# Moving operands read downward, x in tiles of 320 words, and one weight distance a pair, in a two-layer hybrid block on one core

## The chip, the cores and the metric

The kernel runs on one core of a Trainium2 chip. A core has five engines that run beside each other: TensorE (PE, matrix products; the load of a stationary operand is listed as PEld), VectorE (DVE), ScalarE (ACT), GpSimd (POOL) and SyncE (SP, which here only issues transfers). They work on SBUF, an on-chip memory of 128 partitions; PE writes its results to PSUM, which DVE and ACT read. Sixteen DMA engines move data between HBM and SBUF. The metric is the device time of one execution in microseconds (us), smaller being better; several executions are timed and the median is given.

## The reference

The reference is a small language-model block in float32: 256 tokens after 16 learned meta tokens, width 1024, two layers. Cut to what matters:

```python
for li in range(2):
    hn = rms_norm(h, norm_mix_g[li])
    proj = hn @ w_in[li]              # 1024 -> 13312, cut into 12 parts
    o = [retention(...), hgrn2(...), diff_attention(...)]       # each 1024 wide
    y = sum(sigmoid(gate[n]) * (o[n] @ w_branch[li][n]) for n in range(3))
    h = h + y @ w_out[li]
    hn = rms_norm(h, norm_ffn_g[li])
    u = hn @ w_ffn_in[li]                                       # 1024 -> 5632
    c = conv_b + sum(conv_w[j] * shifted(u, 2 - j) for j in range(3))
    gate, val = split(c, 2)
    h = h + (silu(gate) * val) @ w_ffn_out[li]                  # 2816 -> 1024
return rms_norm(h, norm_final_g)[:, meta tokens cut off]
```

Three sequence mixers work on parts of one wide projection; then come their output projections, and a gated feed-forward with a convolution over three tokens. Nearly all arithmetic is in the products with weights, 216 MB of them, each read once.

## The kernel before

**Layout.** Features lie on the 128 partitions and tokens along the free dimension, 272 of them (T). A weight tile is 128 x 128 and is the stationary operand of a product; activations are the moving operand, one column a token. In the second layer the pairs whose results only matter for the last 256 tokens (and two before them, for the convolution) work on 258 columns, from token 14 (T0); the pairs named in FULL keep 272.

**Three products a tile.** To keep float32 accuracy with the fast operand type float32r, each weight tile and each activation is split in two, a rounded part (hi) and the rest (lo). `products` (from line 845) issues for each weight tile three products into the same PSUM region: hi weights by hi activations (line 868), hi weights by lo activations (869) and lo weights by hi activations (870). The main products of all projections run through this function: the wide projection (names rq to m2, numbered in BASE), the branch outputs b0 to b2, wo, the feed-forward input fi (22 pairs j of two tiles) and output fo. The last layer's fo is different: there the weights are the moving operand, 512 columns at a time, and the activations (ghi, glo) the stationary one, so that tokens land on partitions (`final`, from line 1346; products in 1378 to 1380).

**Weights.** They come as a stream in the order of use, eight tiles (512 KB) a chunk. `_Weights.next` (class in line 558) issues the transfer of a chunk into wraw (three buffers), then one ACT instruction that writes whi and one DVE instruction that writes wlo (four buffers each). Where each tile begins in those buffers is worked out in `_places` (line 125): `wants` holds a byte offset, modulo LINE = 256 bytes, for every tile. It is the sum of APART (0, or 96 for pairs that work on 258 columns), 64 more for the branch, wo and fo tiles (BLOCK), and 64 times (k modulo 4), k being the number of the 128 features that are summed over. Gaps are left so that each tile begins there; `_runs` turns the result into strided access patterns. 

**Activations.** The normalised input x is held in six fixed tiles (`xs`, line 725): xh0, xh1, xh2 and xl0 to xl2, each with four k of 272 words. A tile k thus begins 1088 bytes after the one before, which is 64 modulo 256; the weight tiles' 64 bytes a k follow that. The other moving operands (b0hi, b0lo and the like in `split_blocks`, yhi and ylo, ghi and glo) lie in slots, buffers of 4 x 272 words of which there are 14 (SLOTS). Slots also hold q, k and v blocks of the mixers, scratch of the second mixer, and more. A slot tile is taken when it is first written and comes free after its last reader.

**Norms.** A norm's factor rstd is known only after all features are summed, so the first four pairs behind a norm use x without it and are multiplied by rstd afterwards (`evacuate`); for the fifth pair on, `Norm.next` writes x once more with rstd folded in: POOL writes y, ACT xh, DVE xl, for eight k. This happens four times.

**Order.** The program order is made when the kernel is built: every instruction is recorded with an estimated cost and a due time (`plan.key`), and `_Plan.order` picks instructions by readiness and due time, with the number of free buffers of each kind in view. Dependencies between instructions come from `_span`, which gives the range of words that an access pattern touches. The main products follow the fixed list ORDER; the small products of the mixers are woven in between.

Of the kernel before, what the change touches and what calls it, by code (L numbers as in the profile page):

```python
# [12 lines left out]
F32R = mybir.dt.float32r  # L13
# [6 lines left out]
P = 128  # L20
# [3 lines left out]
T = META + SEQ  # L24
D = 1024
KD = D // P
# [8 lines left out]
TAIL = T - 2 * P  # L35
BANK = 512
CHUNK_TILES = 8
SLOTS = 14
LEAD = 6.0
MARGIN = 12.0  # L40
EARLY = 12.0
# [6 lines left out]
BASE = {"rq": 0, "rk": 4, "rv": 8, "rg": 16, "hq": 24, "hf": 32, "hi": 40, "hg": 48,  # L48
        "dq": 56, "dk": 64, "dv": 72, "m0": 80, "m1": 88, "m2": 96}
# [67 lines left out]
LINE = 256  # L117
APART = (0, 96)
BLOCK = 64
ROOM = CHUNK_TILES * P + 2 * LINE // 4  # L120
T0 = META - 2
FULL = ("rk", "rv", "hf", "hi", "dk", "dv")


def _places(depth=DEPTH):

    wants = []
    for li in range(depth):  # L130
        for name, j, k, _ in sum(_turns(li), []):
            if name == "fo" and (li == DEPTH - 1 or j == 3):
                wants.append(None)
                continue
            short = li == DEPTH - 1 and name not in FULL
            wants.append(APART[short] + BLOCK * (name[0] == "b" or name in ("wo", "fo")) + 64 * (k % 4))
    out = []
    for c in range(0, len(wants), CHUNK_TILES):
        at, places = 0, []
        for want in wants[c : c + CHUNK_TILES]:  # L140
            if want is not None:
                at += (want // 4 - at) % (LINE // 4)
            places.append(at)
            at += P
        assert at <= ROOM
        out.append(places)
    return out


def _runs(places):  # L150


    runs = []
    for i, at in enumerate(places):
        if runs and at == runs[-1][1] + runs[-1][2] * P:
            runs[-1][2] += 1
        else:
            runs.append([i, at, 1])
    out = []
    for i, at, n in runs:  # L160
        if out and out[-1][4] == n and (out[-1][3] == 1 or at == out[-1][1] + out[-1][2] * out[-1][3]):
            if out[-1][3] == 1:
                out[-1][2] = at - out[-1][1]
            out[-1][3] += 1
        else:
            out.append([i, at, 0, 1, n])
    return out


def _rope_perm(d):  # L170
# [145 lines left out]
class _Plan:  # L316
# [25 lines left out]

    def _span(self, ap):
        step = ap.ap[0][0]
        lo = ap.offset % step
        hi = lo + 1 + sum((n - 1) * abs(s) for s, n in ap.ap[1:])
        if ap.tensor.name in self.psum:

            lo, hi = lo // BANK * BANK, -(-hi // BANK) * BANK
        return ap.tensor.name, lo, hi  # L350
# [261 lines left out]
def _trace(ctx, tc, plan, a, depth, probe):  # L612
# [9 lines left out]
    wp = ctx.enter_context(tc.tile_pool(name="wp", bufs=3))  # L622
    sp = ctx.enter_context(tc.tile_pool(name="sp", bufs=SLOTS))
    gp = ctx.enter_context(tc.tile_pool(name="gp", bufs=3))
# [11 lines left out]
    def fixed(shape, name, dt=F32):  # L636
        return new(cp, shape, dt, name, 1, name)

    def slot(name, dt=F32):
        return new(sp, [P, 4 * T], dt, "slot", SLOTS, name)  # L640

    def slot4(name, dt=F32):
        return slot(name, dt).rearrange("p (a t) -> p a t", a=4)
# [78 lines left out]
    fmap = fixed([P, DEPTH], "fmap")  # L722
    fixed([P, KD], "step")

    xs = [[fixed([P, KD // 2, T], f"x{n}{i}", F32R) for n in "hl"] for i in range(3)]

    def x_tile(k, folded):
        return tuple(t[:, k % 4, :] for t in xs[1 if k >= 4 else 2 if folded else 0])
    rstd = fixed([P, T], "rstd")


# [168 lines left out]
    def split(hi, lo, x):  # L900
        act.activation(hi, x, AF.Copy)
        tt(lo, x, hi.bitcast(F32), SUB)
# [30 lines left out]
    def split_blocks(name, blocks, t0):  # L933

        his, los = [], []
        for x in blocks:
            hi, lo = slot4(name + "hi", F32R), slot4(name + "lo", F32R)
            split(hi[:, :, t0:], lo[:, :, t0:], x[:, :, t0:])
            his.append(hi)
            los.append(lo)  # L940
        return lambda k: (his[k // 4][:, k % 4, :], los[k // 4][:, k % 4, :])

    for li in range(depth):
        last = li == depth - 1
# [15 lines left out]
        st = {}  # L960
# [441 lines left out]
        for name, j in ORDER:  # L1402
# [18 lines left out]
            elif name[0] == "*":  # L1421
                plan.key = clock[0] - MARGIN
                n = name[1:]
                if n == "b2":
                    blocks = [st["da0"], st["da1"]]
                else:
                    t = st["rg" if n == "b0" else "hg"]
# [6 lines left out]
            if name in BASE:  # L1434
                lo = 0 if name in FULL else t0
                ps = products(lambda k: x_tile(k, norm.folded), name, j, lo)
# [16 lines left out]
                elif name in ("dq", "dk"):  # L1453
                    t = block(f"{name}{j // 2}")
# [12 lines left out]
                elif name in ("hi", "dv"):  # L1467
                    n = name[0] + "v"
# [13 lines left out]
                else:  # L1482
                    t = block(f"{name}{j // 2}")
# [7 lines left out]
            elif name in ("b0", "b1", "b2"):  # L1491
                ps = products(st["x" + name], name, j, t0)
                g = st["m" + name[1]][:, both, t0:]
                yy = block(f"y{j // 2}")[:, two, t0:]
                if name == "b0":
                    tt(yy, ps, g, MUL)
                else:
                    tt(g, ps, g, MUL)
                    tt(yy, yy, g, ADD)
                    if name == "b2":  # L1500
                        if j == 0:
                            st["yhi"] = [slot4("yhi", F32R) for _ in range(2)]
                            st["ylo"] = [slot4("ylo", F32R) for _ in range(2)]
                        split(st["yhi"][j // 2][:, two, t0:], st["ylo"][j // 2][:, two, t0:], yy)
            elif name == "wo":
                hi, lo = st["yhi"], st["ylo"]
                ps = products(lambda k: (hi[k // 4][:, k % 4, :], lo[k // 4][:, k % 4, :]), name, j, t0)
                tt(h[:, both, t0:], h[:, both, t0:], ps, ADD)
                if j == 0:
                    norm = Norm(small[:, S_GF + li * KD : S_GF + (li + 1) * KD])  # L1510
                norm.take([2 * j, 2 * j + 1])
                norm.square([2 * j, 2 * j + 1])
                if j == 3:
                    norm.finish()
            elif name == "fi":
                ps = products(lambda k: x_tile(k, norm.folded), name, j, t0)
                if j % 4 == 0:
                    st.setdefault("ghi", []).append(slot4("ghi", F32R))
                    st.setdefault("glo", []).append(slot4("glo", F32R))
                u = ps  # L1520
                if not norm.folded:
                    u = temp2("two_a")[:, :, t0:]
                    evacuate(u, ps)
                first = META if last else 0
                c = temp2("two_b")
                for f in range(2):
                    ft = j + f * FK
                    w = lambda i: small[:, S_CW + (li * 3 + i) * 2 * FK + ft : S_CW + (li * 3 + i) * 2 * FK + ft + 1]
                    bias = small[:, S_CB + li * 2 * FK + ft : S_CB + li * 2 * FK + ft + 1]
                    act.activation(c[:, f, first:], u[:, f, first - t0 :], AF.Identity, bias=bias, scale=w(2))  # L1530
                    for back in (1, 2):
                        at = max(first, back)
                        stt(c[:, f, at:], u[:, f, at - back - t0 : T - back - t0], w(2 - back), c[:, f, at:], MUL, ADD)
                c = c[:, :, first:]
                act.activation(c[:, 0, :], c[:, 0, :], AF.Silu)
                tt(c[:, 0, :], c[:, 0, :], c[:, 1, :], MUL)
                split(st["ghi"][j // 4][:, j % 4, first:], st["glo"][j // 4][:, j % 4, first:], c[:, 0, :])
            elif last:
                if j == 0:
                    final()  # L1540
            else:
                hi, lo = st["ghi"], st["glo"]
                ps = products(lambda k: (hi[k // 4][:, k % 4, :], lo[k // 4][:, k % 4, :]), name, j)
                if j == 0:
                    norm = Norm(small[:, S_GM + (li + 1) * KD : S_GM + (li + 2) * KD])
                    le_set()
                for ks, x in ([([6], ps[0].unsqueeze(1)), ([7], ps[1].unsqueeze(1))] if j == 3 else [([2 * j, 2 * j + 1], ps)]):
                    if ks[0] == 6:
                        plan.key -= 22 * 0.35
                    if ks[0] == 7:  # L1550
                        norm.rest = True
                        norm.mean()
                        plan.key = clock[0] - 1.0
                    hk = h[:, ks[0] : ks[-1] + 1, :]
                    tt(hk, hk, x, ADD)
                    norm.square(ks)
                    norm.take(ks)
# [20 lines left out]
```

## Time and profile before

| | |
|---|---|
| median of 3 runs | 1329.39 us (1329.1 to 1330.91) |
| profiled execution, span from the first to the last instruction | 1327.6 us |
| PE busy | 1317.0 us, 99% |
| DVE busy | 962.7 us, 73% |
| ACT busy | 816.7 us, 62% |
| POOL busy | 83.6 us, 6% |
| HBM read | 216.16 MB, 164 GB/s over the span |

The profiled execution's own time is its span, and the median of the runs stands 1.8 us above it. A row of the view of groups reads: line, engine, operation, output <- inputs, partitions x elements, count | busy us in total, mean ns of one | idle time of that engine before them and what ended it. In a row of the view of windows stand the window, its length, and for each engine its busy time and in brackets how many instructions ran, then the granted PE clock, the busy share of the DMA engines and their GB/s. In the view of waits a row reads: who waited <- for whom: us in total, times, longest us. In the chain in order of time: start us, us, what. A row for one tile gives minimum, median and maximum duration in ns, then the first and the last start in us.

### The profile page before, as it was taken

What the parts mean: (1) busy time and instruction counts of PE and PEld (TensorE: products, weight loads), DVE (VectorE), ACT (ScalarE), POOL (GpSimd) and SP (SyncE); (2) the same over time, 40 slices, a digit from 0 to 9 for tenths busy, and PEclk for the clock granted to TensorE, in tenths of its full rate; (3) what the DMA queues carried; (4) which work ended last, traced back from release to release, by engine and by line L of the source; (5) the groups of instructions that cost most, each with busy time, mean ns of one, the idle gap of its engine ahead of it and who ended that gap; (6) DMA issues with size and microseconds to landing.
All of it is one profiled execution on the core that took longest, in us unless ns stands there. A gap on an engine that the chain in (4) does not pass through costs nothing.

```text
span 1327.6 us, 28926 instructions
## 1 busy us (share of the span) xinstructions
PE 1317.0 (99%) x11862; PEld 1288.8 (97%) x11862; DVE 962.7 (73%) x1630; ACT 816.7 (62%) x1374; POOL 83.6 (6%) x161
## 2 busy tenths in 40 slices
PE   9999999999999999999999999999999999999998
PEld 9999999999999999999999999999999999999986
DVE  7675777697586789886574757776985867898753
ACT  6747454756676567666456474557565775767643
POOL 5000000001010020000030000000011100200000
PEclk9999999999999999999999999999999999999999
DMA  7644543443534545555555445444445446465653
GB/s 272 195 146 155 170 150 128 143 143 129 188 131 158 177 157 176 187 168 186 175 175 181 155 159 161 160 140 143 143 149 175 142 162 199 135 208 189 201 182 109
DMA packets 60755, 219.07 MB, mean 165 GB/s; under 512 B 6864, under 2 KB 6992, under 8 KB 60624
## 3 DMA queue, kind: packets, MB, share of 16 engines
q1 hardware_dynamic: 60336, 216.71, 49.1%
q8 instruction: 93, 1.52, 0.5%
q10 hardware_dynamic: 288, 0.52, 0.1%
q14 instruction: 38, 0.31, 0.1%
HBM read 216.16 MB, written 1.05 MB: 164 GB/s over the span
## 4 chain that ended last, share of the span: by engine, by line
PE 95%; DVE 3%; issue 1%; DMA 0%; ACT 0%; SPq 0%; DVEq 0%
PE main L868 28%; PE main L870 27%; PE main L869 27%; PE fo L1380 2%; PE fo L1378 2%; PE fo L1379 2%; PE lev L1059 1%; DVE two_b L553 1%; PE ds L1243 1%; PE ms L553 1%; PE do L553 1%; DVE wlo L553 1%; PE ro L553 1%; PE ho L553 1%; PE vt L553 1%
## 5 line engine op out<-in xcount | busy, mean ns | idle before, releaser
L868 PE MATMUL main<-xh,whi 128*128 128x272 f32 (+1 forms) x2368 | 693.2, 293 | 0.2 <-ACT whi L553 0.2
L870 PE MATMUL main<-xh,wlo 128*128 128x272 f32 (+1 forms) x2368 | 680.5, 287 | 0.8 <-DVE wlo L553 0.7
L869 PE MATMUL main<-xl,whi 128*128 128x272 f32 (+1 forms) x2368 | 671.6, 284 | 1.6 <-DVE xl L553 1.5
L553 DVE TENSOR_TENSOR wlo<-wraw,whi 128x1024 fp32r<-128x1024 f32 (+1 forms) x408 | 497.1, 1223 | 200.9 <-ACT whi L553 199.8
L553 ACT ACTIVATE whi<-wraw 128x1024 fp32r<-128x1024 f32 (+1 forms) x408 | 426.6, 1048 | 229.5 <-PE main L869 162.2
L869 PEld LDWEIGHTS main<-xl,whi 128*128 128x128 f32 x2368 | 448.9, 190 | 2.5 <-DVE xl L553 2.1
L868 PEld LDWEIGHTS main<-xh,whi 128*128 128x128 f32 x2368 | 445.6, 188 | 2.5 <-issue 0.7
L870 PEld LDWEIGHTS main<-xh,wlo 128*128 128x128 f32 x2368 | 444.6, 188 | 2.2 <-DVE wlo L553 2.1
L553 DVE SCALAR_TENSOR_TENSOR two_b<-main,small,two_b 128x256 f32<-128x256 f32 (+2 forms) x144 | 65.3, 488 | 29.1 <-ACT two_b L553 27.4
L553 POOL TENSOR_TENSOR y<-h,rstd 128x272 f32<-128x272 f32 x32 | 34.6, 1114 | 316.7 <-ACT rstd L553 316.7
L553 ACT ACTIVATE two_b<-main,small 128x272 f32<-128x272 f32 (+1 forms) x72 | 37.3, 567 | 26.8 <-PE main L870 26.6
L870 PE MATMUL main<-ghi,wlo 128*128 128x272 f32 x176 | 51.0, 290 | 0.0
L868 PE MATMUL main<-ghi,whi 128*128 128x272 f32 x176 | 50.9, 289 | 0.0
L869 PE MATMUL main<-glo,whi 128*128 128x272 f32 x176 | 50.2, 285 | 0.0
L553 ACT ACTIVATE vsrc<-main 128x544 f32<-128x544 f32 x24 | 15.0, 626 | 39.4 <-PE main L870 39.2
L868 PE MATMUL main<-b0hi,whi 128*128 128x272 f32 (+1 forms) x128 | 38.1, 298 | 0.0
L868 PE MATMUL main<-b1hi,whi 128*128 128x272 f32 (+1 forms) x128 | 38.1, 298 | 0.0
L870 PE MATMUL main<-yhi,wlo 128*128 128x272 f32 (+1 forms) x128 | 36.7, 286 | 0.0
L870 PE MATMUL main<-b2hi,wlo 128*128 128x272 f32 (+1 forms) x128 | 36.6, 286 | 0.0
L870 PE MATMUL main<-b1hi,wlo 128*128 128x272 f32 (+1 forms) x128 | 36.6, 286 | 0.0
L870 PE MATMUL main<-b0hi,wlo 128*128 128x272 f32 (+1 forms) x128 | 36.6, 286 | 0.0
L868 PE MATMUL main<-yhi,whi 128*128 128x272 f32 (+1 forms) x128 | 36.5, 285 | 0.0
(244 smaller groups left out, 1936.4 us busy)
## 6 DMA issues: line engine op xcount, KB each, us to landing
wraw<-in_w SPq DMA_DIRECT2D x402, 512.0 KB, 3.4
h<-in_h SPq DMA_DIRECT2D x4, 272.0 KB, 5.2
dec<-in_dec SPq DMA_DIRECT2D x2, 544.0 KB, 5.4
wraw<-in_w SPq DMA_DIRECT2D x4, 256.0 KB, 4.6
const<-in_const SPq DMA_DIRECT2D x1, 937.0 KB, 6.1
gain<-in_gl SPq DMA_DIRECT2D x1, 512.0 KB, 6.1
out<-y ACTq DMA_DIRECT2D x2, 256.0 KB, 2.8
out<-y SPq DMA_DIRECT2D x2, 256.0 KB, 2.7
```

The source lines that it names most:

```text
L553: self.plan.add(self.name, lambda: f(*args, **kw), cost, outs, ins, args[2] if method == "activation" else None)
L868: nc.tensor.matmul(o, wh, hi, start=first, stop=False)
L869: nc.tensor.matmul(o, wh, lo, start=False, stop=False)
L870: nc.tensor.matmul(o, wl, hi, start=False, stop=last)
L1059: nc.tensor.matmul(o, keys, x, start=True, stop=True)
L1243: nc.tensor.matmul(ss[m][:, at : at + nk], q[half, hd, q0 : q0 + P], k[half, hd, :nk], start=True, stop=True)
L1378: nc.tensor.matmul(o, gh, wh, start=False, stop=False)
L1379: nc.tensor.matmul(o, gl, wh, start=False, stop=False)
L1380: nc.tensor.matmul(o, gh, wl, start=False, stop=end)
```

## The change

The x tiles get room for 320 words a k (WIDE), of which 272 are used, so that a k begins 1280 bytes after the one before, a multiple of 256. The weight tiles of the wide projection and of fi no longer step by 64 bytes a k; those of the wide projection begin at APART, and in fi each pair j has its own offset from a list (SPREAD): the multiples of 16 bytes up to 240, then six more from 8 on in steps of 40. The x tiles grow by 4608 bytes a partition; there is one slot of 4352 bytes less.

The new function `_down` makes an access pattern that goes through the last dimension from its end to its beginning. All moving operands of the main products are taken through it, where they are written (by ACT and DVE) and where they are read (by PE). The last token therefore lies at the lowest address, and PE reads from the highest address down. The stationary ghi and glo of the last stage stay as they were. `_span` is mended so that a negative step gives the right range.

```diff
-SLOTS = 14
+SLOTS = 13
...
+SPREAD = [16 * i for i in range(16)] + [8 + 40 * i for i in range(6)]
+WIDE = 320
...
+            if name in BASE or name == "fi":
+                wants.append((SPREAD[j] if name == "fi" else APART[short]) % LINE)
+                continue
             wants.append(APART[short] + BLOCK * (name[0] == "b" or name in ("wo", "fo")) + 64 * (k % 4))
...
+def _down(t):
+
+
+    step, n = t.ap[-1]
+    return bass.AP(t.tensor, t.offset + (n - 1) * step, [list(x) for x in t.ap[:-1]] + [[-step, n]])
...
-        lo = ap.offset % step
+        lo = ap.offset % step + sum((n - 1) * min(s, 0) for s, n in ap.ap[1:])
...
-    xs = [[fixed([P, KD // 2, T], f"x{n}{i}", F32R) for n in "hl"] for i in range(3)]
+    xs = [[fixed([P, KD // 2, WIDE], f"x{n}{i}", F32R)[:, :, :T] for n in "hl"] for i in range(3)]
 
     def x_tile(k, folded):
-        return tuple(t[:, k % 4, :] for t in xs[1 if k >= 4 else 2 if folded else 0])
+        return tuple(_down(t[:, k % 4, :]) for t in xs[1 if k >= 4 else 2 if folded else 0])
...
-            hi, lo = slot4(name + "hi", F32R), slot4(name + "lo", F32R)
+            hi, lo = (_down(slot4(name + n, F32R)) for n in ("hi", "lo"))
...
-                            st["yhi"] = [slot4("yhi", F32R) for _ in range(2)]
-                            st["ylo"] = [slot4("ylo", F32R) for _ in range(2)]
+                            st["yhi"] = [_down(slot4("yhi", F32R)) for _ in range(2)]
+                            st["ylo"] = [_down(slot4("ylo", F32R)) for _ in range(2)]
...
-                    st.setdefault("ghi", []).append(slot4("ghi", F32R))
-                    st.setdefault("glo", []).append(slot4("glo", F32R))
+                    for n in ("ghi", "glo"):
+                        t = slot4(n, F32R)
+                        st.setdefault(n, []).append(t if last else _down(t))
```

## The prediction

> **What bounds the kernel now.** I read the page first, its shares of busy time, the clock line and the shares of the chain that ended last:
>
> ```profile
> span 1327.6 us, 28926 instructions
> PE 1317.0 (99%) x11862; PEld 1288.8 (97%) x11862; DVE 962.7 (73%) x1630; ACT 816.7 (62%) x1374; POOL 83.6 (6%) x161
> PEclk9999999999999999999999999999999999999999
> PE 95%; DVE 3%; issue 1%; DMA 0%; ACT 0%; SPq 0%; DVEq 0%
> ```
>
> PE carries 95% of the chain, at full granted clock in all 40 slices. A busy PE may still wait inside, so the view of waits for PE alone comes next:
>
> ```profile
> PE main L869 <- DVE xl L553: 1.5, 1, 1.5
> PE warm L553 <- POOL ones_d L553: 1.0, 1, 1.0
> PE main L870 <- DVE wlo L553: 0.7, 3, 0.3
> PE lev L1059 <- issue: 0.5, 1, 0.5
> ```
>
> Nearly nothing: PE is the bound because it has work, and the time is the number of its products times the spacing of their starts. So I counted products. The view of groups with shapes kept apart, for line 869 (one of the three products of a weight tile; 868 and 870 have the same counts):
>
> ```profile
> L869 PE MATMUL main<-xl,whi 128*128 128x272 f32 x1536 | 437.3, 285 | 0.1
> L869 PE MATMUL main<-xl,whi 128*128 128x258 f32 x832 | 234.3, 282 | 1.5 <-DVE xl L553 1.5
> L869 PE MATMUL main<-glo,whi 128*128 128x272 f32 x176 | 50.2, 285 | 0.0
> L869 PE MATMUL main<-b0lo,whi 128*128 128x272 f32 x64 | 18.2, 285 | 0.0
> L869 PE MATMUL main<-b0lo,whi 128*128 128x258 f32 x64 | 18.0, 281 | 0.0
> ```
>
> b1, b2 and y have 64 of each shape as b0 has. So products of 272 columns: 3 x (1536 + 176 + 4 x 64) = 5904; of 258: 3 x (832 + 4 x 64) = 3264; together 9168. All of them get a moving operand that is read downward. One ns on each is 9.2 us, 0.69% of the time; 0.2%, about what a measurement of this kernel tells from no change, is 2.7 us or 0.29 ns a product.
>
> Their spacing is not their duration (285 ns; they overlap), but window length over count. Windows inside the stages that hold nothing else, first for line 869 alone (272 columns, then 258), then for the 512-column products of the last stage:
>
> ```profile
> 520.00:660.00 140.00, 106.24 (x375) 1.00 0.56 184
> 1165.00:1255.00 90.00, 70.64 (x251) 1.00 0.60 198
> 1260.00:1318.00 58.00, 57.79 (x251) 1.00 0.48 154
> ```
>
> 140/375/3 = 124.4 ns, 90/251/3 = 119.5 ns, 58/251 = 231 ns. What would they be if only columns counted? The fp32 products, which run as two passes each, tell. From the chain in order of time (four passes of 144 columns, two of 272), with the groups that give their columns:
>
> ```profile
> 108.33 0.49 PE px L553 x4
> 481.56 0.46 PE ms L553 x2
> L553 PE MATMUL px<-hq,hf 128*128 128x144 f32 x32 | 5.9, 285 | 0.0
> L553 PE MATMUL ms<-sum,ones_d 128*128 128x272 f32 x8 | 2.6, 405 | 0.0
> ```
>
> 122.5 and 230 ns a pass: 0.84 ns a column and 1.5 ns fixed. The main products take half of that a column, as 512 against 272 columns shows ((231 - 124.4)/240 = 0.44). At 0.42 ns a column and 1.5 ns fixed, 272, 258 and 512 columns would need 115.7, 109.9 and 216.5 ns. **The surplus** is 8.7, 9.6 and 14.5 ns; on the main products 5904 x 8.7 + 3264 x 9.6 = 83 us. It is absent where a moving word is taken only every 0.84 ns, though a weight load runs beside every pass there too. I read it as reads of the moving operand at full rate that lose turns, probably to the weight load of the next product; no view shows this directly.
>
> **The change part by part.**
>
> *Reading downward.* It adds and removes no product. Its price is what the surplus becomes. From below: nothing excludes that it goes, -83 us. From above: if a word read downward were taken at the fp32 pace, a 272-column product would cost 230 ns and a 258-column one 218, +105.6 x 5904 + 98.5 x 3264 = +945 us. The nearest rows are the main products' own, since operand type, columns and weight load stay: a surplus of 8.7 at one distance and 9.6 at another (the second layer's weight tiles begin 96 bytes further and its reads 14 words, 56 bytes, further: 40 bytes apart). Today both streams ascend, so an offset was there to be chosen; read downward against an ascending weight load, the moving operand passes every offset in each product, whichever one it began at, and an average is paid. I take 9.6 ns for all: +0.9 x 5904 = +5.3 us. The 14.5 ns of the 512-column products, whose tiles have another arrangement, is a farther row, kept for the range.
>
> *One distance a pair; x in tiles of 320 words.* Before, weight tiles of k step 64 bytes to follow x's tiles of 272 words (1088 bytes, 64 past a multiple of 256). Now x steps 1280 bytes, a multiple of 256, and weights of the x products lie back to back: the distance, modulo 256 bytes, is the same as before in the big projection (0 or 96 at the weights), and 22 different ones in fi. If distance is swept anyway, this is nothing; if it isn't, fi's 2 x 22 pairs x 48 = 2112 products get offsets between good and bad. Two offsets known differ by 0.9 ns: -1.9 to +1.9 us, taken as 0 and kept.
>
> *Splitting of weights.* The same 8 tiles a chunk, one ACT and one DVE instruction, written in one piece where they had four. The last stage's chunks are in one piece already; DVE windows 520 to 600, then 1268 to 1312:
>
> ```profile
> L553 DVE TENSOR_TENSOR wlo<-wraw,whi 128x1024 fp32r<-128x1024 f32 x28 | 34.1, 1219 | 1.9 <-ACT whi L553 1.9
> L553 DVE TENSOR_TENSOR wlo<-wraw,whi 128x1024 fp32r<-128x1024 f32 x17 | 20.8, 1226 | 24.6 <-ACT whi L553 24.6
> ```
>
> The same to 7 ns: 0. DMA issues and the queues on SP are untouched.
>
> *Splits written downward.* Every writer of xh, xl, ghi, glo (first layer), b0 to b2 and y, on ACT and DVE. They lie beside PE, except in two places of some 25 us (x folded with rstd), where the chain runs on DVE: in the first DVE is busy 25.21 of 26 us.
>
> ```profile
> 484.00:510.00 26.00, 25.21 (x41) 1.00 0.36 123
> L553 DVE SCALAR_TENSOR_TENSOR xl<-y,small,xh 128x272 fp32r<-128x272 f32 x8 | 3.8, 500 | 0.0
> L553 DVE TENSOR_TENSOR glo<-two_b,ghi 128x272 fp32r<-128x272 f32 x3 | 1.3, 440 | 0.0
> ```
>
> If a downward operand made them twice as long, 5.1 us a place, 10 in all, with no cover left; a gain is excluded, since the words to be written stay the same number. Either way they are neighbouring words written one after the other, so I take 0. [...]
>
> *13 slots.* It costs only where all 14 were held. Going by the first and last instruction of each slot tile, never more than 12 are live. One place that full is the down projection: 22 tiles of ghi and glo in fours are 12 slots, read until 675.5; the next two, y, are first written at 679.9:
>
> ```profile
> L870 PE MATMUL main<-ghi,wlo x176: 282/289/292, 609.4 to 675.5; 128*128 128x272 f32 x176
> L553 POOL TENSOR_TENSOR y<-h,rstd x8: 768/976/1759, 679.9 to 687.7; 128x272 f32<-128x272 f32 x8
> ```
>
> No wait in PE's list above comes from a slot, and a thirteenth is still free: 0; with a late dec or da tile the planner may shift some small work, 0 to 3 us.
>
> **Sum.** The profiled span of 1327.6 us has 1.8 us to the median of the runs, 1329.4. 1327.6 + 5.3 = 1332.9; with the same 1.8 around it 1334.7, say 1335, a loss of 0.4%. With the small bounds (fi 1.9, DVE 10, slots 3) this case's own range is 1331 to 1350.
>
> **The rivals.**
>
> *Opposite streams clash less (faster).* Two streams that ascend can run beside each other in the same part of the memory for a while; two in opposite directions pass at once. If passing costs a quarter less, the surplus gives 83/4 = 21 us: 1309; half, 41 us: 1288; all, 1247. It decides as soon as a product gains 0.29 ns. For it: the surplus is there whether 258 or 272 columns are read. Against: passes come more often the faster the streams part, and the total time in the same part stays about what it is.
>
> *Direction doesn't count (same).* If the surplus is no clash, but the cost of fetching at full rate, it goes with words, not with direction: 8.7 against 14.5 ns for 272 against 512 columns grows with the words. Then the sum is 1329 plus or minus 2.7. [...]
>
> *Downward is dearer (slower).* If clashes come at each pass and none is cheaper, the surplus rises to that of the 512-column products: +5.8 x 5904 + 4.9 x 3264 = 50 us: 1380. For it: those products read at no chosen offset. Against: they also read more words.
>
> *Downward breaks the full rate.* The fp32 pace, 1329 + 945 = 2274. Against: the words lie next to each other as before; only the sign of the step is new, and no instruction in this trace has it. [...]
>
> **How the numbers follow.** Likeliest case, an averaged clash: 0.36. Faster: 0.29 (0.07 of it below 1295). Same: 0.10. Dearer: 0.17 (0.04 of it above 1390). Half the rate: 0.08. So slower 0.61, same 0.10, faster 0.29. The range 1295 to 1390 leaves out 0.07 + 0.04 + 0.08 = 0.19.
>
> **What would show it.** The window of the first layer's fi and down projection, and of the second layer's fi: counts of line 869 per window give the spacing. 125.3 and 119.5 ns are right; below 124.1 and 119.2 the faster rival; 130 and 124 the dearer one; over 200 the last. Between the fi pairs of one layer the spacing should not differ if the distance is swept. The xl and glo groups stay at 500 and 440 ns if the downward writes are free. A PE wait that ends on a slot's reader would show the 13 slots. The prediction is wrong above all if the surplus has another cause than the one assumed: then it may move either way by tens of us with everything else as told.

## The result and the profile after

The changed kernel takes 1333.69 us (median of 7 runs, 1332.43 to 1334.39) against 1330.04 us for the kernel before on the same chips (7 runs, the three of the table before the change among them, 1329.10 to 1330.91). The ratio is 1.0028, with a 95% interval of 1.0019 to 1.0038: slower by 3.7 us, where 5.3 were forecast. The execution that was profiled is the longest of its seven (1334.39), so the spans differ by more than the medians. The page of the changed kernel, the lines that answer to those of before:

```profile
span 1332.6 us, 28929 instructions
PE 1322.1 (99%) x11862; PEld 1293.6 (97%) x11862; DVE 962.8 (72%) x1630; ACT 816.5 (61%) x1374; POOL 83.7 (6%) x161
PEclk9999999999999999999999999999999999999999
PE 95%; DVE 3%; issue 1%; ACT 1%; DMA 0%; SPq 0%; DVEq 0%
```

The span is longer by 5.0 us, PE's busy time by 5.1, and DVE, ACT and POOL agree with before to 0.2 us. PE has the same number of instructions at the same clock. Its waits (products of lines 868 to 870 are 880 to 882 now):

```profile
PE main L881 <- DVE xl L565: 1.2, 1, 1.2
PE lev L1071 <- issue: 1.1, 2, 0.7
PE warm L565 <- POOL ones_d L565: 1.0, 1, 1.0
PE main L882 <- DVE wlo L565: 0.5, 2, 0.3
```

In sum they are as long as before (4.0 us, 4.1 before). So the time went into the spacing of the products. The two windows of line 869 (881 now) in which the prediction looked for its sign:

```profile
520.00:660.00 140.00, 107.83 (x373) 1.00 0.55 183
1165.00:1255.00 90.00, 70.51 (x250) 1.00 0.59 199
```

They give 125.1 and 120.0 ns, where 125.3 and 119.5 were forecast. A window cut at whole pairs is finer. One from the start of the first product of fi's pair 6 to that of pair 21 holds 15 pairs x 48 = 720 products and little else. Pair 6 has some other work between its products, so these means stand up to 1 ns above those of the clean pairs (124.7 ns before, in the first layer). For one line of the three the row counts 241, since one product begun earlier still runs at its edge. First the two rows of the kernel before (first layer with 272 columns, second with 258), then those of the changed kernel:

```profile
513.14:603.21 90.07, 68.11 (x241) 1.00 0.56 182
1166.53:1252.73 86.20, 67.68 (x241) 1.00 0.60 198
```

```profile
514.32:604.90 90.58, 69.43 (x241) 1.00 0.56 183
1171.17:1257.57 86.40, 67.91 (x241) 1.00 0.59 198
```

Length over 720: 125.1 and 119.7 ns before, 125.8 and 120.0 after. Taking the difference of the starts of neighbouring main products all through the two traces (5578 such differences at 272 columns, 3094 at 258), the means go from 124.65 to 125.06 and from 119.37 to 120.04 ns: +0.41 x 5904 + 0.67 x 3264 = 2.4 + 2.2 = 4.6 of the span's 5.0 us.

The new distances are visible too. Two neighbouring pairs of the first layer's fi in the changed kernel, 48 products each (pairs 8 and 9):

```profile
526.69:532.67 5.98, 4.61 (x17) 1.00 0.66 217
532.67:538.74 6.07, 4.67 (x17) 1.00 0.55 190
```

124.6 and 126.5 ns: at 272 columns the offset of the weight tile still matters, with two levels. From pair 7 on, six pairs of 15 lie at the upper one, and one between. In the second layer every one of the 22 pairs takes 119.9 to 120.1 ns.

### The profile page after: what moved, and what is told of

Same layout as the page of the kernel before. It is cut to its first block, busy times and chain, and to the rows that moved or that the text cites. A ratio compares the mean times of both kernels' runs of the same rounds, so it can differ in the third digit from the quotient of the medians.

```text
span 1332.6 us, 28929 instructions
## 1 busy us (share of the span) xinstructions
PE 1322.1 (99%) x11862; PEld 1293.6 (97%) x11862; DVE 962.8 (72%) x1630; ACT 816.5 (61%) x1374; POOL 83.7 (6%) x161
## 4 chain that ended last, share of the span: by engine, by line
PE 95%; DVE 3%; issue 1%; ACT 1%; DMA 0%; SPq 0%; DVEq 0%
PE main L880 28%; PE main L882 27%; PE main L881 27%; PE fo L1390 2%; PE fo L1392 2%; PE fo L1391 2%; PE lev L1071 1%; DVE two_b L565 1%; PE ds L1255 1%; PE do L565 1%; PE ms L565 1%; PE ro L565 1%; PE ho L565 1%; PE vt L565 1%; DVE wlo L565 1%
## 5 line engine op out<-in xcount | busy, mean ns | idle before, releaser
L881 PE MATMUL main<-xl,whi 128*128 128x272 f32 (+1 forms) x2368 | 679.9, 287 | 1.2 <-DVE xl L565 1.2
L881 PE MATMUL main<-b1lo,whi 128*128 128x272 f32 (+1 forms) x128 | 36.6, 286 | 0.0
```

The costliest lines, as they stand in the source:

```text
L881: nc.tensor.matmul(o, wh, lo, start=False, stop=False)
```

## Direction or layout

The first question is which part of the change costs. Two kernels do one part each.

**Downward alone.** The kernel before with `_down` on the same operands (shown for x) and the mended `_span`; x stays in tiles of 272 words, the weights step by 64 bytes a k, 14 slots:

```diff
     def x_tile(k, folded):
-        return tuple(t[:, k % 4, :] for t in xs[1 if k >= 4 else 2 if folded else 0])
+        return tuple(_down(t[:, k % 4, :]) for t in xs[1 if k >= 4 else 2 if folded else 0])
```

> The kernel before with the moving operands written and read downward, and nothing else changed: x in tiles of 272 words, weight tiles stepping by 64 bytes a k, 14 slots. Clash theory (a moving read at full rate loses turns to the weight load of the next product; read downward, every offset is passed, so the starting offset does not count): nearly the time of the whole change, 1333 to 1336 us, with 120.0 ns a product of 258 columns and 124.5 to 126.5 at 272. Layout theory (the loss comes from the offsets in fi and the slot, not from the direction): 1329 to 1331 us.

Measured: 1332.38 us against 1329.70, ratio 1.0022 (1.0013 to 1.0031). Its two windows:

```profile
513.76:603.78 90.02, 69.48 (x241) 1.00 0.58 183
1169.08:1255.41 86.33, 67.84 (x241) 1.00 0.62 197
```

125.0 ns at 272 columns, as before (125.1), and 119.9 at 258, 0.2 more; over all products the means are 124.92 and 120.03. The direction by itself costs 2.7 us. By the means over all products it is 0.27 x 5904 = 1.6 us at 272 columns, nearly all outside the window shown, and 0.66 x 3264 = 2.2 us at 258; PE's waits are 1.1 us shorter in this trace (3.0 against 4.1 us). The time lies between the two expectations: the layout theory fails, and the clash theory asked for a little more.

**The layout alone, upward.** The changed kernel with `_down` made to return its argument:

```diff
 def _down(t):
-    step, n = t.ap[-1]
-    return bass.AP(t.tensor, t.offset + (n - 1) * step, [list(x) for x in t.ap[:-1]] + [[-step, n]])
+    return t
```

> The changed kernel with the moving operands upward again: x in tiles of 320 words, 22 distances in fi, 13 slots. Clash theory: read upward, the offset counts in both layers, so the 44 fi pairs differ from one another, by 3 ns a product or more between best and worst, at 258 columns too, where the downward reads gave 120.0 at every offset; the total lies within 5 us of the kernel before, 1326 to 1334. Fetch theory (the surplus is what fetching the moving words costs by itself): the fi pairs do not differ by more than 1 ns. Layout theory: about the time of the whole change, 1333 to 1336.

Measured: 1325.83 us, ratio 0.9972 (0.9960 to 0.9983): faster than the kernel before by 3.9 us. Two pairs of the second layer's fi (11 and 15):

```profile
1191.54:1197.19 5.65, 4.48 (x17) 1.00 0.60 195
1214.38:1220.30 5.92, 4.51 (x17) 1.00 0.56 178
```

117.7 and 123.3 ns, 5.6 apart, for the same products with the weight tile begun elsewhere (176 and 240 bytes past a multiple of 256). In the first layer the pairs lie between 123.4 and 127.6. So, read upward, the offset counts in both layers, and the layout is a gain: with x at multiples of 256 bytes the wide projection takes 123.7 ns at 272 columns where it took 124.6. (In fi the 22 offsets lose some of that: 125.7 ns over the first layer's pairs, 124.7 before.) Read downward the same layout is worth nothing (1333.69 with it, 1332.38 without). Against this kernel, reading downward costs some 7.5 us: 3.9 below the kernel before against 3.7 above it.

**One constant distance, upward.** If the offsets in fi matter, one good offset should beat 22. The upward kernel again, with one more edit:

```diff
-                wants.append((SPREAD[j] if name == "fi" else APART[short]) % LINE)
+                wants.append(APART[short])
```

> The changed kernel with the moving operands upward again and one constant distance in fi too (0 bytes at 272 columns, 96 at 258) in place of 22. From the fi pairs of the upward run with 22 distances: 123.4 ns at offset 0 against a mean of 125.7 over the 22 pairs of the first layer, 118.0 at 96 against 119.6 in the second; 1056 products each, so 2.4 + 1.7 = 4 us less than that run, about 1322 us, faster than the kernel before by some 0.6%. If the distances in fi did not matter upward, 1326 us as there.

Measured: 1323.12 us, ratio 0.9957 (0.9943 to 0.9970): 6.2 us faster than before, and some 1 us above what was expected; with its variant of 260 columns below, the fastest kernel here that computes the block.

```profile
510.81:599.94 89.13, 68.76 (x241) 1.00 0.58 185
1161.53:1246.42 84.89, 66.71 (x241) 1.00 0.61 201
```

123.8 and 117.9 ns. Against the kernel before, which reads upward at the same chosen offset, what is new for PE is that x no longer drifts by 64 bytes a k. In the trace of before, the weight load of the next product begins with the present product (at 560.06 us both, 0.12 us before the product that it is for). So, while the last product of one k ran, the first weight tile of the next k was loaded; before, that tile lay 64 bytes further than the others did, relative to the words being read. Now it has the same distance.

The traces bear this out. In the trace of before, the start after a product of lo weights by hi activations (line 870) on x at 272 columns came 127.6 ns later where the next tile was one of the next k, and 124.9 ns where it was not (some 700 cases each, longer gaps left out). In this kernel the two are 123.4 and 123.5. The products whose moving operand lies in a slot still drift by 64 bytes a k, and they still have 127.6 and 124.9 here. So at 272 columns the extra cost of the step to the next k, 2.7 ns, belongs to the drift. Where x itself begins is not the reason there: in the trace of before each of the six products of a k has the same spacing to 0.1 ns in all eight k (fi, 272 columns), though x begins at 0, 64, 128 and 192 bytes in turn. Why the other starts became shorter too, by 1.4 ns, is not shown.

## What the surplus is

The prediction put 8.7 and 9.6 ns a product, beyond the time it estimated for the columns alone, down to clashes of the moving read with the weight load. These kernels change one of the two reads at a time. They leave the number, size and order of all instructions, but with the full weights or activations left out they no longer compute the block. Each was run once.

**Weight loads from one word.**

```diff
+def _one(t):
+    return bass.AP(t.tensor, t.offset, [list(x) for x in t.ap[:-1]] + [[0, t.ap[-1][1]]])
...
-            wh, wl = weights.next()
+            wh, wl = (_one(x) for x in weights.next())
```

> The kernel before, but each weight load of the main products takes all its 128 columns from one word, so that it touches one place of the memory instead of 128 words. The products are therefore with a wrong weight; their number, sizes and order stay. Clash theory: with the load out of the way the surplus goes, 272 columns fall from 124.4 to 116 to 118 ns and 258 from 119.5 to 110 to 112, the whole by up to 70 us where DVE keeps up. Fetch theory: 124.4 and 119.5 stay, the time within 5 us. Handover theory (the next product waits until its weight load is through): 124.4 and 119.5 stay.

Measured: 1319.45 us (1329.70 before); windows:

```profile
514.19:604.25 90.06, 68.42 (x241) 1.00 0.56 183
1159.60:1242.97 83.37, 66.77 (x241) 1.00 0.63 204
```

125.1 ns at 272 columns, nothing gone; 115.8 at 258, some 4 ns less. The clash theory wanted 116 to 118 and 110 to 112; the two theories by which nothing changes miss the 258 columns.

**Moving columns from one word.**

```diff
-            hi, lo = (x[:, t0:] for x in xs(k))
+            hi, lo = (_one(x[:, t0:]) for x in xs(k))
```

> The kernel before, but each main product takes all its moving columns from one word of each partition; weight loads stay as they are. The results are therefore wrong; number, sizes and order of the products stay. Clash theory and fetch theory: the surplus goes, 116 to 118 and 110 to 112 ns, up to 70 us less. Handover theory: 124.4 and 119.5 ns stay, the time within 5 us.

Measured: 1265.74 us, 64 us less.

```profile
488.16:572.54 84.38, 66.89 (x241) 1.00 0.61 195
1108.52:1189.43 80.91, 65.89 (x241) 1.00 0.66 210
```

117.2 and 112.4 ns; a clean pair is at 116.3 and 111.8. Nearly the whole surplus goes, so it depends on the moving words, and a next product that waits for its weight load is not the cause.

**Every moving word twice.** Half the words, the same columns, full weight loads:

```diff
+def _twice(t):
+    step, n = t.ap[-1]
+    return bass.AP(t.tensor, t.offset, [list(x) for x in t.ap[:-1]] + [[step, n // 2], [0, 2]])
...
-            hi, lo = (x[:, t0:] for x in xs(k))
+            hi, lo = (_twice(x[:, t0:]) for x in xs(k))
```

> The kernel before, but each main product reads half as many moving words, every one twice, so 272 or 258 columns come from 136 or 129 neighbouring words; the results are wrong, the number, sizes and order of products and loads stay. A surplus that goes with the words fetched is halved: about 120 ns at 272 and 114 to 115 at 258, 40 us less. One that goes with the columns stays: 124.4 and 119.5, the time within 5 us. A clash with the load only where the streams meet lies between: 118 to 124.

Measured: 1262.49 us, 67 us less.

```profile
487.81:571.90 84.09, 66.96 (x241) 1.00 0.62 195
1105.43:1186.22 80.79, 66.00 (x241) 1.00 0.66 210
```

116.8 and 112.2 ns, 115.8 and 111.7 in a clean pair against the 115.7 and 109.9 estimated for the columns alone: not half of the surplus but nearly all of it is gone, with the full weight load beside it. All three expectations missed this. It agrees with the fp32 passes of the prediction, 122.5 ns for 144 columns and 230 for 272, so 0.84 ns a word: by the estimate made from them, the surplus exists in these kernels only where a new word is wanted every 0.42 ns. It does not tell a cost of fetching from a clash with the load, since with a word for two columns a lost turn may cost nothing.

**One-word loads at 22 offsets, upward and downward.** The layout of the changed kernel with `_one` on the weights, first with `_down` as an identity, then with `_down` as it is.

> Upward, x in tiles of 320 words, 22 distances in fi, and each weight load of the main products takes all 128 columns from the first word of its tile, so the products are with a wrong weight. Clash theory: the load now sits in one line, and what it costs depends on where that line lies against the moving words, so the 22 pairs of a layer differ by 3 ns or more, or all fall towards 116 and 110 ns. Fetch theory (the moving words cost their surplus by themselves): all pairs of a layer agree within 1 ns and keep a surplus of 5 ns or more.

> The same with the moving operands downward, that is the changed kernel with one-word weight loads (wrong weights again). Clash theory: without a sweeping load the direction no longer matters, so each layer has the spacings of the upward run with one-word loads, to 1 ns. Theory that a downward fetch is dearer by itself: 120.0 ns at 258 columns and 124.5 to 126.5 at 272 stay, as in the changed kernel.

Measured: 1316.74 us upward and 1329.17 downward (1329.35 before). Windows upward:

```profile
512.41:602.23 89.82, 68.63 (x241) 1.00 0.58 183
1156.99:1240.18 83.19, 66.61 (x241) 1.00 0.64 204
```

and downward:

```profile
511.80:601.67 89.87, 69.11 (x241) 1.00 0.58 183
1165.97:1252.37 86.40, 67.77 (x241) 1.00 0.62 197
```

At 272 columns 124.8 both ways, and the two levels of the downward pairs are gone; at 258 columns 115.5 upward and 120.0 downward. So with the load confined to one word the place of that word hardly counts any more, as the fetch theory had it, though not within its 1 ns (upward, 19 of the 22 pairs of the second layer lie at 115.0 to 115.4, three at 117.3 to 118.3). The downward read is dearer by itself at 258 columns, by 4.5 ns. What the full weight load adds to that differs: downward at 258 columns nothing (120.0 either way), downward at 272 columns 0 or 2 ns by the offset, upward between -1 and +3 ns at 272 and +3 to +8 at 258. How often a load from one word reads is not shown. A kernel without any load was not tried, so a clash that does not depend on the place of the load stays possible.

**Where the read begins.** At 258 columns the downward read begins at the second of four words, so I moved the second layer's short products to 260 columns, from token 12:

```diff
-T0 = META - 2
+T0 = META - 4
```

> The changed kernel with the second layer's short products at 260 columns, from token 12, in place of 258 from token 14: a downward read then begins at the last of four neighbouring words that start at a multiple of 16 bytes, and an upward one at the first; at 258 both began in the middle of four. If the 5 ns that downward costs more at 258 columns come from where the read begins, 260 columns take 116 to 118 ns; if they go with the direction at this length, 120.8 (two columns of 0.42 ns more than 120.0).

> The upward kernel with x in tiles of 320 words and one constant distance, with 260 columns from token 12 in the second layer. If the start within four words is what counts, the products of 260 columns change by other than the 0.8 ns of two columns against the 118.0 of 258 in fi; if not, 118.9 and 2 to 3 us more than that kernel at 258.

Measured: 1334.33 us downward (1333.69 at 258 columns) and 1323.03 upward in the kernel with one constant distance (1323.12). Windows of the second layer, downward and then upward:

```profile
1170.81:1257.51 86.70, 67.93 (x241) 1.00 0.62 196
```

```profile
1161.02:1246.30 85.28, 67.45 (x241) 1.00 0.61 199
```

120.4 and 118.4 ns. Downward, 20 of the 22 pairs are at 119.9 to 120.3, two at 122.1 and 123.4; upward 118.3 for most. The place in the four words is not the reason: begun at the last word of a group of four, the downward read stays at 120. Nor did the two columns add their 0.8 ns: downward none, upward 0.5. Downward times seem to come in steps (258 and 260 columns both 120.0; 272 columns 124.5 or 126.6), and why is open.

## Why the prediction was right or wrong

**The sum.** 1334.7 was forecast, 1333.69 came; the loss is 0.28% and not 0.4%. The direction of the result and the bound (PE, spacing of 9168 products, no new wait) were right. Its reasons were right only in part.

**The price of reading downward** was put at +0.9 ns on the 272-column products and 0 on the 258-column ones. Measured with all parts: +0.41 and +0.67. The total, 4.6 us against 5.3, was near because the two misses cancel, which is luck. What failed is the step that took the surplus of the 258-column products as the value of an averaged offset: the downward price is one of its own at each length. The one-word loads show it, where there is no sweep to average: 4.5 ns more than upward at 258 columns, nothing at 272. Where it comes from is open.

**"Every offset is passed, whichever one it began at"** holds at 258 columns, where 22 offsets gave 119.9 to 120.1 ns, and fails at 272 (124.5 or 126.6). That the two streams both ascended before was an assumption: no run shows in which order a weight load goes through its tile, and no run turned that order round.

**The surplus as a clash with the weight load.** As a clash that depends on where the load reads, not the main cause: with one-word loads 9 ns stay at 272 columns and 5.7 at 258, with half the moving words 0.1 and 1.8. The part of the sentence that held is "at full rate"; whether the rest is the fetching itself or a clash of another kind is open. The load does add something, as the offsets of the upward run show: 117.7 to 123.3 ns with nothing else different.

**One distance a pair and x in 320 words, taken as 0 with 1.9 us either way.** Downward it was about +1 us: the first layer's fi has a mean of 125.4 ns over the pairs against 124.5 at the lower level, 0.9 x 1056 = 1.0 us; with the second layer's pairs all alike, the bound of 1.9 us held. Upward the same layout is worth -3.9 us, beyond the bound I gave: I compared offsets of whole pairs and overlooked the step between one k and the next, which the wider tiles remove from all x products.

**Splits written downward, weights in one piece, 13 slots: 0 each.** Right. Two groups and a wait of the changed kernel:

```profile
L565 DVE SCALAR_TENSOR_TENSOR xl<-y,small,xh 128x272 fp32r<-128x272 f32 x32 | 19.8, 657 | 0.2 <-ACT xh L565 0.2
L565 DVE TENSOR_TENSOR glo<-two_b,ghi 128x272 fp32r<-128x272 f32 x22 | 9.6, 437 | 0.0
ACT yhi L565 <- DVE y L565: 3.7, 7, 0.7
```

The first two before:

```profile
L553 DVE SCALAR_TENSOR_TENSOR xl<-y,small,xh 128x272 fp32r<-128x272 f32 x32 | 19.9, 659 | 0.2 <-ACT xh L553 0.2
L553 DVE TENSOR_TENSOR glo<-two_b,ghi 128x272 fp32r<-128x272 f32 x22 | 9.6, 436 | 0.0
```

So in these two forms a downward operand on DVE cost nothing measurable: 657 ns against 659, and 437 against 436. yhi, which is written into a slot, waits for its input y, and none of PE's waits ends on a reader of a slot.

**The rivals.** Opposite streams that clash less: no, the time rose by 3.7 us. Direction doesn't count: refuted by downward alone, 1.0022 with 1.0013 as the lower end, though only just; its reading of the surplus as a cost of fetching fits the one-word loads better (9 ns of surplus left at 272 columns, 5.7 at 258). Dearer, 1380: no. Half the rate: no, 120.0 ns at 258 columns and not 218.

## What to carry to other kernels

Where PE is the bound and nothing waits, look at the spacing of the products' starts against an estimate of what their columns need: here that estimate left some 9 ns of 125 in every product, while the views showed PE 99% busy and 4.1 us of waits. In this kernel the spacing depended on where the moving operand and the weight tile lie: by the offset alone 117.7 to 123.3 ns at 258 columns, read upward. One distance for every x product, the step to the next k included, took 0.4% off the time (1323.12 us against 1329.35). A single total can come out right for reasons that are half wrong; only kernels that change one read at a time told the parts apart.

## What was not expected of the hardware

- The spacing of 272 columns falls from 125.1 to 116.8 ns, and of 258 from 119.7 to 112.2, if each moving word is used for two neighbouring columns, with the instructions and their order the same.
- A moving operand read downward costs 120.0 ns at 258 columns, wherever the weight tile lies and whether its load reads 128 words or one; upward it is 115.0 with a one-word load and 117.7 to 123.3 with a full one. At 260 columns it is 120.0 as well.
- At 272 columns the downward spacing has two levels, 124.5 and 126.6 ns, by the weight tile's offset; with one-word loads the upper one is gone. Why these levels and steps exist was not found.
